# Instance norm on one core: stores and loads in turns on one queue, and the gamma columns and Sqrt table prepared while the first unit lands

## The chip, the cores and the metric

One core of one Trainium2 chip. The time is the device time of one execution in microseconds (us), on the slowest core, which here is the only one. Executions of one kernel agree closely: the kernel before took 626.88 to 627.35 us in its own four runs. A run is called fast when it is not more than 1.5% above the fastest of its kernel, and only fast runs are compared. A ratio of two kernels is the mean time of the one's fast runs over the mean time of the other's fast runs of the same rounds, so it is not quite the ratio of the medians that are quoted beside it.

## The reference

```python
# x: 4 x 8 x 16 x 256 x 256 float32, gamma: 8 x 16 float32
mu    = x.mean(axis=(3, 4), keepdims=True)
var   = ((x - mu) ** 2).mean(axis=(3, 4), keepdims=True)
out   = (x - mu) / np.sqrt(var + 1e-5) * gamma[None, :, :, None, None]
```

Each of 512 channels has 65,536 values, which are normalised by their own mean and variance. 134.22 MB are read and 134.22 MB are written, each value once.

## The kernel before

A *unit* is 16 channels: a tile of 128 partitions x 8,192 float32 (4 MB), eight partitions to a channel. There are 32 units and six slots in SBUF. For each unit VectorE (DVE) sums the rows, ScalarE (ACT) sums the squares, a small matmul adds up the eight partitions of a channel, a few tiny steps give the scale, and DVE normalises the tile in place. Then the tile is stored, and a load that reuses its slot is issued.

```python
    def load(u, queue):
        queue.dma_start(out=slots[u % AHEAD][:], in_=xv[u])       # AHEAD = 6

    for u in range(AHEAD):
        load(u, nc.scalar if u in (1, 3) else nc.sync)
        if u == 1:
            nc.sync.dma_start(out=g_row[:], in_=gv[None, :])
    # ... constants cut
    for u in range(U):                                            # U = 32
        t = slots[u % AHEAD]
        nc.vector.reduce_sum(out=st[:, u, 0:1], in_=t[:], axis=AX.X)
        square = nc.scalar.activation(out=junk[:], in_=t[:], func=ACTF.Square,
                                      accum_out=st[:, u, 1:2])
        if u == 0:
            gamma_columns()              # a copy, 8 matmuls, a copy
        # ... matmul ps, nvar, Sqrt std, reciprocal rstd, scale cut
        nc.vector.tensor_scalar(out=t[:], in0=t[:], scalar1=ps[:, 0:1],
                                scalar2=scale[:, u : u + 1], op0=ALU.add, op1=ALU.mult)
        nc.scalar.dma_start(out=ov[u], in_=t[:])
        if u + AHEAD < U:
            load(u + AHEAD, nc.sync)
```

So all stores go out on the ACT queue, and all loads but two on the SP queue. A load waits until the store of the unit that had its slot six units earlier has landed.

Of the kernel before, what the change touches and what calls it, by code (L numbers as in the profile page):

```python
# [1 line left out]

# [4 lines left out]

F32 = mybir.dt.float32
U8 = mybir.dt.uint8
ALU = mybir.AluOpType  # L10
ACTF = mybir.ActivationFunctionType
AX = mybir.AxisListType


@with_exitstack
def kernel(
    ctx: ExitStack,
    tc: tile.TileContext,
    x: bass.AP,
    gamma: bass.AP,  # L20
    out: bass.AP,
):
    nc = tc.nc
    B, G, C, H, W = x.shape
    P = nc.NUM_PARTITIONS
    HW = H * W
    n_ch = B * G * C
    S = 8
    K = P // S
    F = HW // S  # L30
    U = n_ch // K
    NG = (G * C) // K
    AHEAD = 6
    assert HW % S == 0 and (G * C) % K == 0

    xv = x.rearrange("b g c h w -> (b g c h w)").rearrange("(u p f) -> u p f", p=P, f=F)
    ov = out.rearrange("b g c h w -> (b g c h w)").rearrange("(u p f) -> u p f", p=P, f=F)
    gv = gamma.rearrange("g c -> (g c)")

    data = ctx.enter_context(tc.tile_pool(name="data", bufs=1))  # L40
    singles = ctx.enter_context(tc.tile_pool(name="singles", bufs=1))
    psum = ctx.enter_context(tc.tile_pool(name="psum", bufs=4, space=bass.MemoryType.PSUM))
    ctx.enter_context(tc.manual_schedule())

    slots = [data.tile([P, F], F32, name=f"xt{i}") for i in range(AHEAD)]

    def load(u, queue):
        queue.dma_start(out=slots[u % AHEAD][:], in_=xv[u])  # L48


    g_row = singles.tile([1, G * C], F32, name="g_row")
    for u in range(AHEAD):
        load(u, nc.scalar if u in (1, 3) else nc.sync)
        if u == 1:
            nc.sync.dma_start(out=g_row[:], in_=gv[None, :])


    eps_t = singles.tile([P, 1], F32, name="eps_t")
    nc.gpsimd.memset(eps_t[:], 1e-5)
    one = singles.tile([1, 1], F32, name="one")  # L60
    nc.gpsimd.memset(one[:], 1.0)
    navg = singles.tile([P, K, S], F32, name="navg")
    nc.gpsimd.memset(navg[:], -1.0 / HW)  # L63
    nc.gpsimd.affine_select(  # L64
        out=navg[:], in_=navg[:], pattern=[[-S, K], [0, S]], compare_op=ALU.is_ge,
        fill=0.0, base=0, channel_multiplier=1,
    )
    nc.gpsimd.affine_select(  # L68
        out=navg[:], in_=navg[:], pattern=[[S, K], [0, S]], compare_op=ALU.is_ge,
        fill=0.0, base=S - 1, channel_multiplier=-1,  # L70
    )
    navg_w = navg[:].rearrange("p k s -> p (k s)")
    g_rep = singles.tile([1, NG, K, S], F32, name="g_rep")
    g_ps = psum.tile([P, NG], F32, name="g_ps", bufs=1)
    g_col = singles.tile([P, NG], F32, name="g_col")

    def gamma_columns():
        nc.vector.tensor_copy(  # L78
            out=g_rep[:],
            in_=g_row[:].rearrange("o (n k) -> o n k", n=NG).unsqueeze(3).to_broadcast([1, NG, K, S]),  # L80
        )
        for n in range(NG):
            nc.tensor.matmul(  # L83
                out=g_ps[:, n : n + 1],
                lhsT=g_rep[:, n].rearrange("o k s -> o (k s)"),
                rhs=one[:],
                start=True, stop=True,
            )
        nc.vector.tensor_copy(out=g_col[:], in_=g_ps[:])  # L89

    junk = singles.tile([P, F], U8, name="junk")

    st = singles.tile([P, U, 2], F32, name="st")
    nvar = singles.tile([P, U], F32, name="nvar")
    std = singles.tile([P, U], F32, name="std")
    rstd = singles.tile([P, U], F32, name="rstd")
    scale = singles.tile([P, U], F32, name="scale")

    squares = []
    for u in range(U):  # L100
        t = slots[u % AHEAD]
        nc.vector.reduce_sum(out=st[:, u, 0:1], in_=t[:], axis=AX.X)  # L102
        square = nc.scalar.activation(  # L103
            out=junk[:], in_=t[:], func=ACTF.Square, accum_out=st[:, u, 1:2],
        )
        if u:

            tc.declare_no_dep(square.ins, squares[-1].ins, reason="junk, ordered by the root between")
        squares.append(square)
        if u == 0:  # L110
            gamma_columns()
        ps = psum.tile([P, 2], F32, name="ps")
        nc.tensor.matmul(out=ps[:], lhsT=navg_w, rhs=st[:, u], start=True, stop=True)  # L113
        nc.vector.tensor_scalar(  # L114
            out=nvar[:, u : u + 1], in0=ps[:, 0:1], scalar1=ps[:, 0:1],
            scalar2=ps[:, 1:2], op0=ALU.mult, op1=ALU.add,
        )
        nc.scalar.activation(  # L118
            out=std[:, u : u + 1], in_=nvar[:, u : u + 1], func=ACTF.Sqrt,
            bias=eps_t[:], scale=-1.0,  # L120
        )
        nc.vector.reciprocal(out=rstd[:, u : u + 1], in_=std[:, u : u + 1])  # L122
        g = u % NG
        nc.vector.tensor_mul(  # L124
            out=scale[:, u : u + 1], in0=rstd[:, u : u + 1], in1=g_col[:, g : g + 1],
        )
        nc.vector.tensor_scalar(  # L127
            out=t[:], in0=t[:], scalar1=ps[:, 0:1], scalar2=scale[:, u : u + 1],
            op0=ALU.add, op1=ALU.mult,
        )  # L130
        nc.scalar.dma_start(out=ov[u], in_=t[:])
        if u + AHEAD < U:
            load(u + AHEAD, nc.sync)


# [1 line left out]
_INS = ['x', 'gamma']  # L137
_OUTS = [((4, 8, 16, 256, 256), 'float32')]


# [23 lines left out]
```

## Time and profile before

626.95 us (median of three runs). The profiled execution has a span of 625.1 us.

| | before |
|---|---|
| busy share of the span: DVE, ACT, PE | 71%, 38%, 3% |
| share of the 16 DMA engines' span, both queues | 52.8% + 46.8% |
| mean rate over the span | 429 GB/s |
| DVE work for one unit, and the interval between units late in the run | about 15 us, 19.35 us |

The lines below are from the page of the kernel before: the busy share of the DMA engines (in tenths; 9 is 90% or more) and the rate in 40 slices of the span, the queue table (queue, kind: packets, MB, share of the 16 engines' span), four groups of instructions (count, busy us and mean ns, then the idle time before them) and the issues (KB each, median us from issue to landing). Queue q10 is ACT's, q1 is SP's.

```profile
DMA  8999999999999999999999999999999999999998
GB/s 371 434 436 419 419 436 436 436 436 436 435 436 435 428 426 436 426 436 436 434 436 436 434 434 432 428 432 426 436 436 434 436 436 434 434 436 428 428 436 359
DMA packets 9220, 268.46 MB, mean 429 GB/s; under 512 B 1025, under 2 KB 1026, under 8 KB 1026
...
q10 hardware_dynamic: 4896, 142.61, 52.8%
q1 hardware_dynamic: 4322, 125.83, 46.8%
...
L102 DVE TENSOR_REDUCE st<-xt 128x1 f32<-128x8192 f32 x32 | 277.9, 8684 | 110.2 <-DMA xt<-in_x_dram 110.2
...
L127 DVE TENSOR_SCALAR xt<-xt,ps,scale 128x8192 f32<-128x8192 f32 x32 | 145.6, 4550 | 1.2
...
L118 ACT ACT_TABLE_LOAD x1 | 1.3, 1283 | 6.8 <-DVE nvar L114 6.8
...
L103 ACT ACT_TABLE_LOAD x1 | 1.3, 1283 | 1.7 <-PEq L148 1.7
...
out_dram<-xt ACTq DMA_DIRECT2D x32, 4096.0 KB, 64.1
xt<-in_x_dram SPq DMA_DIRECT2D x30, 4096.0 KB, 29.0
```

Read them together: the transfers fill the run from end to end, and no compute engine comes near that. The only way to be faster is to lose less at the start, at the end, or inside the stream of packets.

Two lines of the timeline show when the first unit is handled (start us, us, engine, line, operation, and the idle time before):

```profile
22.61 8.69 DVE L102 TENSOR_REDUCE st<-xt 128x1 f32<-128x8192 f32 x1 [22.61 <-DMA xt<-in_x_dram]
...
38.51 4.55 DVE L127 TENSOR_SCALAR xt<-xt,ps,scale 128x8192 f32<-128x8192 f32 x1
```

### The profile page before, as it was taken

What the parts mean: (1) busy time and instruction counts of PE and PEld (TensorE: products, weight loads), DVE (VectorE), ACT (ScalarE), POOL (GpSimd) and SP (SyncE); (2) the same over time, 40 slices, a digit from 0 to 9 for tenths busy, and PEclk for the clock granted to TensorE, in tenths of its full rate; (3) what the DMA queues carried; (4) which work ended last, traced back from release to release, by engine and by line L of the source; (5) the groups of instructions that cost most, each with busy time, mean ns of one, the idle gap of its engine ahead of it and who ended that gap; (6) DMA issues with size and microseconds to landing.
All of it is one profiled execution on the core that took longest, in us unless ns stands there. A gap on an engine that the chain in (4) does not pass through costs nothing.

```text
span 625.1 us, 628 instructions
## 1 busy us (share of the span) xinstructions
PE 21.4 (3%) x80; PEld 19.5 (3%) x80; DVE 442.9 (71%) x162; ACT 239.9 (38%) x98; POOL 1.3 (0%) x9
## 2 busy tenths in 40 slices
PE   0020000000000000000000000000000000000000
PEld 0020000000000000000000000000000000000000
DVE  0569999999898767867668676686766877667710
ACT  0435555544444423444224442244432444323400
POOL 0000000000000000000000000000000000000000
DMA  8999999999999999999999999999999999999998
GB/s 371 434 436 419 419 436 436 436 436 436 435 436 435 428 426 436 426 436 436 434 436 436 434 434 432 428 432 426 436 436 434 436 436 434 434 436 428 428 436 359
DMA packets 9220, 268.46 MB, mean 429 GB/s; under 512 B 1025, under 2 KB 1026, under 8 KB 1026
## 3 DMA queue, kind: packets, MB, share of 16 engines
q10 hardware_dynamic: 4896, 142.61, 52.8%
q1 hardware_dynamic: 4322, 125.83, 46.8%
q14 instruction: 2, 0.02, 0.0%
HBM read 134.22 MB, written 134.22 MB: 429 GB/s over the span
## 4 chain that ended last, share of the span: by engine, by line
DMA 62%; DVE 30%; PE 2%; issue 1%; ACT 1%; SPq 0%; ACTq 0%
DMA xt<-in_x_dram 55%; DVE st L102 24%; DMA out_dram<-xt 7%; DVE xt L127 5%; PE ps L113 2%; DVE nvar L114 1%; PE g_ps L83 1%; ACT std L118 0%; ACT L118 0%; DVE rstd L122 0%; DVE scale L124 0%; DVE g_rep L78 0%; SPq L48 0%; ACTq L118 0%
## 5 line engine op out<-in xcount | busy, mean ns | idle before, releaser
L102 DVE TENSOR_REDUCE st<-xt 128x1 f32<-128x8192 f32 x32 | 277.9, 8684 | 110.2 <-DMA xt<-in_x_dram 110.2
L103 ACT ACTIVATE junk<-xt 128x8192 uint8<-128x8192 f32 x32 | 224.9, 7030 | 266.1 <-DMA xt<-in_x_dram 212.1
L127 DVE TENSOR_SCALAR xt<-xt,ps,scale 128x8192 f32<-128x8192 f32 x32 | 145.6, 4550 | 1.2
L118 ACT ACTIVATE std<-nvar,eps_t 128x1 f32<-128x1 f32 x32 | 9.4, 295 | 76.0 <-DVE nvar L114 76.0
L113 PE MATMUL ps<-st,navg 128*128 128x2 f32 x64 | 17.9, 349 | 536.4 <-DVE st L102 536.4
L113 PEld LDWEIGHTS ps<-st,navg 128*128 128x128 f32 x64 | 16.0, 311 | 538.2 <-issue 538.2
L114 DVE TENSOR_SCALAR nvar<-ps 128x1 f32<-128x1 f32 x32 | 9.2, 286 | 23.4 <-PE ps L113 23.4
L122 DVE RECIPROCAL rstd<-std 128x1 f32<-128x1 f32 x32 | 5.2, 164 | 12.9 <-ACT std L118 12.9
L103 ACT ACTIVATION_READ_ACCUMULATOR junk<-xt 128x1 f32 x32 | 6.0, 186 | 0.0
L124 DVE TENSOR_TENSOR scale<-rstd,g_col 128x1 f32<-128x1 f32 x32 | 5.1, 159 | 1.1
L83 PE MATMUL g_ps<-one,g_rep 1*128 1x1 f32 x16 | 3.5, 346 | 32.0 <-DVE g_rep L78 32.0
L83 PEld LDWEIGHTS g_ps<-one,g_rep 1*128 1x128 f32 x16 | 3.5, 325 | 32.0 <-issue 32.0
L118 ACT ACT_TABLE_LOAD x1 | 1.3, 1283 | 6.8 <-DVE nvar L114 6.8
L89 DVE COPY g_col<-g_ps 128x8 f32<-128x8 f32 x1 | 0.2, 166 | 3.7 <-PE g_ps L83 3.7
L103 ACT ACT_TABLE_LOAD x1 | 1.3, 1283 | 1.7 <-PEq L148 1.7
L78 DVE COPY g_rep<-g_row 1x1024 f32<-1x1024 f32 x1 | 0.7, 670 | 0.0
L64 POOL TENSOR_SCALAR_AFFINE_SELECT navg<-navg 128x128 f32<-128x128 f32 x1 | 0.4, 405 | 0.1
L68 POOL TENSOR_SCALAR_AFFINE_SELECT navg<-navg 128x128 f32<-128x128 f32 x1 | 0.4, 399 | 0.1
L63 POOL MEMSET navg<- 128x128 f32 x1 | 0.2, 222 | 0.0
L148 POOL MEMSET const-bfloat16-1.0<- 128x1 bf16 x1 | 0.1, 102 | 0.0
L148 POOL MEMSET const-uint8-127<- 128x1 uint8 x1 | 0.1, 102 | 0.0
L148 POOL MEMSET const-float32-0.0<- 128x1 f32 x1 | 0.1, 99 | 0.3 <-issue 0.3
(3 smaller groups left out, 0.3 us busy)
## 6 DMA issues: line engine op xcount, KB each, us to landing
out_dram<-xt ACTq DMA_DIRECT2D x32, 4096.0 KB, 64.1
xt<-in_x_dram SPq DMA_DIRECT2D x30, 4096.0 KB, 29.0
xt<-in_x_dram ACTq DMA_DIRECT2D x2, 4096.0 KB, 31.4
g_row<-in_gamma_dram SPq DMA_DIRECT2D x1, 0.5 KB
```

The source lines that it names most:

```text
L64: nc.gpsimd.affine_select(out=navg[:], in_=navg[:], pattern=[[-S, K], [0, S]], compare_op=ALU.is_ge, fill=0.0, base=0, channel_multiplier=1,)
L68: nc.gpsimd.affine_select(out=navg[:], in_=navg[:], pattern=[[S, K], [0, S]], compare_op=ALU.is_ge, fill=0.0, base=S - 1, channel_multipli ...
L78: nc.vector.tensor_copy(out=g_rep[:], in_=g_row[:].rearrange("o (n k) -> o n k", n=NG).unsqueeze(3).to_broadcast([1, NG, K, S]),)
L83: nc.tensor.matmul(out=g_ps[:, n : n + 1], lhsT=g_rep[:, n].rearrange("o k s -> o (k s)"), rhs=one[:], start=True, stop=True,)
L102: nc.vector.reduce_sum(out=st[:, u, 0:1], in_=t[:], axis=AX.X)
L103: square = nc.scalar.activation(out=junk[:], in_=t[:], func=ACTF.Square, accum_out=st[:, u, 1:2],)
L113: nc.tensor.matmul(out=ps[:], lhsT=navg_w, rhs=st[:, u], start=True, stop=True)
L114: nc.vector.tensor_scalar(out=nvar[:, u : u + 1], in0=ps[:, 0:1], scalar1=ps[:, 0:1], scalar2=ps[:, 1:2], op0=ALU.mult, op1=ALU.add,)
L118: nc.scalar.activation(out=std[:, u : u + 1], in_=nvar[:, u : u + 1], func=ACTF.Sqrt, bias=eps_t[:], scale=-1.0,)
L122: nc.vector.reciprocal(out=rstd[:, u : u + 1], in_=std[:, u : u + 1])
L124: nc.vector.tensor_mul(out=scale[:, u : u + 1], in0=rstd[:, u : u + 1], in1=g_col[:, g : g + 1],)
L127: nc.vector.tensor_scalar(out=t[:], in0=t[:], scalar1=ps[:, 0:1], scalar2=scale[:, u : u + 1], op0=ALU.add, op1=ALU.mult,)
```

## The change

Its intent: keep loads and stores in one strict order, so that neither runs ahead of the other, and take the gamma columns and the Sqrt table load out of the first unit's way.

```diff
-    def load(u, queue):
-        queue.dma_start(out=slots[u % AHEAD][:], in_=xv[u])
+    def load(u):
+        nc.sync.dma_start(out=slots[u % AHEAD][:], in_=xv[u])

-    for u in range(AHEAD):
-        load(u, nc.scalar if u in (1, 3) else nc.sync)
-        if u == 1:
-            nc.sync.dma_start(out=g_row[:], in_=gv[None, :])
+    nc.scalar.dma_start(out=g_row[:], in_=gv[None, :])
+    for u in range(AHEAD - 1):
+        load(u)
 ...
+    nc.scalar.activation(out=root_eps[:], in_=eps_t[:], func=ACTF.Sqrt)
+    # the body of gamma_columns() stands here now, in front of the loop
 ...
-        if u == 0:
-            gamma_columns()
 ...
-        nc.scalar.dma_start(out=ov[u], in_=t[:])
-        if u + AHEAD < U:
-            load(u + AHEAD, nc.sync)
+        nc.sync.dma_start(out=ov[u], in_=t[:])
+        if u + AHEAD - 1 < U:
+            load(u + AHEAD - 1)
```

The SP queue now holds load 0 to load 4, store 0, load 5, store 1, load 6 and so on.

## The prediction

> **What bounds the kernel now.** The transfers. The page's queue table gives 52.8% + 46.8% = 99.6% of the 16 engines' span, 268.46 MB at a mean 429 GB/s. DVE is busy 71%, ACT 38%. By the timeline a unit takes DVE about 15 us (8.69 reduce, 4.55 normalise, small steps) of the 19.35 us between units late in the run.
>
> By the trace's DMA records each engine moves 512 packets of 32 KB. The first starts at 2.0 us, the last round at 621.8. The period per packet is 1,210.2 ns with three kinds of queueing alike: two queues of loads (22 to 41 us), loads on one and stores on the other (80 to 560 us), stores alone on one queue (after 584 us). So a second queue buys no rate. The floor is 2.0 + 512 x 1.2102 = 621.6 us, plus about 2.3 us until the last store is seen to be complete: 624 us, against a span of 625.1. Only some 1.2 us is lost: 0.6 us in the very first packets (up to 2,032 ns) and 0.65 us in load packets at 44.7 to 48 us, just when the first store starts (up to 1,872 ns).
>
> The Trainium skill, "DMA: Bandwidth & Descriptors", section "Issuing engines are not separate DMA queues", says that DMAs run on the same 16 engines whoever issues them, and that more issuers save only issue time. The trace agrees (1,210 ns with one queue or two; an issue costs 0.33 us).
>
> **What the change moves.**
> - Unit 0 lands alone, at about 12 us (estimate: 2.0 + 8 x 1.21 + 0.6) instead of 22.6.
> - The gamma columns and one of two 1.28 us table loads leave unit 0's chain (reduce ends 31.3, nvar starts 36.1): about 6 us. Unit 0 is normalised near 28 us instead of 43.1. But loads are queued to about 50 us, so the transfers gain nothing.
> - Stores and loads stand in one FIFO. Load u+6 waits for store u to land; behind store u are load u+5 and store u+1, about 17 us of work after 2 us latency, so the engines don't run dry. DVE doesn't hold the FIFO either: eight transfers (77 us) lie between load u+1 and store u+1.
> - All engines now read for 9.7 us, then write for 9.7 us. Pure stretches of each kind ran at full rate before; the turn between them inside one queue is not shown. That is the risk.
>
> **Critical path.** Almost none of the saving is on it. At best the 0.65 us at the first store vanishes.
>
> **Prediction: 626.4 us, 8 in 10 between 625.4 and 629.0.** Faster by over 2%: 0.01; within 2%: 0.93; slower: 0.06.
>
> **What would show it.** Queue table: nearly all bytes on the SP queue, again about 99.6%, mean 428 to 430 GB/s. First DVE reduce at about 12 us, first normalise over near 28. One table load instead of two. Issue to landing: stores about 38 us instead of 64, loads still about 29. DVE and ACT busy times unchanged. Packet period 1,210 ns, no dip at the turns.
>
> **What would make it wrong.** Each turn costing time: 0.2 us at 64 turns adds 13 us and passes 2%. An engine gap at the boundary of two transfers of one queue. SP blocked so long that the queue empties (the rate would dip every 19 us). A faster result needs packets below 1,210 ns, which nothing shows.

## The result

631.98 us, median of four runs (631.34 to 632.25), against 626.93. The ratio is 1.0078, with a 95% interval of 1.006 to 1.0095. That is within 2%, as forecast, but about 5 us slower and 3 us above the upper end of the stated range. The profiled run has a span of 630.1 us, 5.0 more than before.

The answering lines of the page after:

```profile
DMA  8999999999999999999999999999999999999996
GB/s 366 433 435 416 431 422 435 429 431 435 420 431 437 424 435 419 433 437 431 439 431 433 433 433 422 435 435 435 433 433 433 435 433 433 433 433 433 433 433 289
DMA packets 9221, 268.46 MB, mean 426 GB/s; under 512 B 1025, under 2 KB 1026, under 8 KB 1026
...
q1 hardware_dynamic: 9216, 268.44, 99.3%
...
L102 DVE TENSOR_REDUCE st<-xt 128x1 f32<-128x8192 f32 x32 | 277.9, 8684 | 108.9 <-DMA xt<-in_x_dram 108.9
...
L125 DVE TENSOR_SCALAR xt<-xt,ps,scale 128x8192 f32<-128x8192 f32 x32 | 145.6, 4551 | 1.2
...
L73 ACT ACT_TABLE_LOAD x1 | 1.3, 1283 | 1.4 <-PEq L146 1.4
...
xt<-in_x_dram SPq DMA_DIRECT2D x32, 4096.0 KB, 29.3
out_dram<-xt SPq DMA_DIRECT2D x32, 4096.0 KB, 38.9
```

And of the timeline after:

```profile
13.16 8.69 DVE L102 TENSOR_REDUCE st<-xt 128x1 f32<-128x8192 f32 x1 [6.55 <-DMA xt<-in_x_dram]
...
23.64 4.55 DVE L125 TENSOR_SCALAR xt<-xt,ps,scale 128x8192 f32<-128x8192 f32 x1
```

Everything on the compute side came as intended: the first unit is ready at 28.2 us instead of 43.1, and one table load is left. The transfers are just as full, by the share of busy time (99.3%). But a packet that is held up counts as busy all the while, so that share can't show the loss. The rate can: 426 instead of 429 GB/s, and the last slice fell from 359 to 289.

The end of the run shows the loss most plainly. The view by stretches of time gives from:to, length, busy times of the engines, clock, DMA share and GB/s. First the kernel before, then the kernel after:

```profile
612.00:620.00 8.00, 0.00 (x0) 0.00 (x0) 0.00 (x0) 0.00 (x0) 0.00 (x0) 1.00 1.00 430
620.00:622.00 2.00, 0.00 (x0) 0.00 (x0) 0.00 (x0) 0.00 (x0) 0.00 (x0) 1.00 1.10 475
622.00:624.00 2.00, 0.00 (x0) 0.00 (x0) 0.00 (x0) 0.00 (x0) 0.00 (x0) 1.00 0.12 49
624.00:626.00 2.00, 0.00 (x0) 0.00 (x0) 0.00 (x0) 0.00 (x0) 0.00 (x0) 1.00 0.03 8
626.00:628.00 2.00, 0.00 (x0) 0.00 (x0) 0.00 (x0) 0.00 (x0) 0.00 (x0) 1.00 0.00 0
```

```profile
620.00:622.00 2.00, 0.00 (x0) 0.00 (x0) 0.00 (x0) 0.00 (x0) 0.00 (x0) 1.00 1.06 459
622.00:624.00 2.00, 0.00 (x0) 0.00 (x0) 0.00 (x0) 0.00 (x0) 0.00 (x0) 1.00 0.95 410
624.00:626.00 2.00, 0.00 (x0) 0.00 (x0) 0.00 (x0) 0.00 (x0) 0.00 (x0) 1.00 0.34 147
626.00:628.00 2.00, 0.00 (x0) 0.00 (x0) 0.00 (x0) 0.00 (x0) 0.00 (x0) 1.00 0.27 115
```

Packets are counted where they start, so single stretches can pass 1.00. What counts is the shape: before, the last packet of the stores is over by 623.6 us. After, by the packets' own start and length, 11 of the 16 engines still work at 624 us, 6 at 626 and 3 at 628. The 16 DMA engines have come apart.

The trace's landing records tell how far. The Trainium skill, "DMA: Bandwidth & Descriptors", section "Why a DMA increments its semaphore by 16 and not by 1", says that each of the engines that carry a transfer posts its own increment when its share has landed. The trace agrees: each of the 64 large transfers has 16 landing records. The *spread* of a transfer is the time from its first to its last record. This table gives the spread, in us, of the transfer that had landed last by the time named:

```
                by 50   100   150   200   250   300   400   500 us   at the end   last store landed, first and last engine
before          1.72  0.34  0.32  1.01  0.95  0.86  0.90  0.86       0.87         623.07  623.94
after           0.64  1.18  1.56  2.86  2.97  3.91  4.98  4.98       4.97         623.97  628.94
```

With this the 5.0 us are accounted for: the first engine finishes 0.90 us later than before, the last one 4.10 us further behind it (4.97 less 0.87), and from the last landing to the end of the program it is 1.13 us in both.

What puts the engines apart? Not idle time: between 20 and 620 us an engine stands without a packet for about 0.01 us in all, in both kernels, so neither an empty queue nor a gap between two transfers costs anything. The packets themselves take longer. Nearly every packet of 32 KB takes 1,213 ns in both kernels. Call one *stretched* when it took over 1,240 ns, and add up what it took over 1,213, divided by 16 engines. Before, that is 1.26 us: 0.58 in the first packets of the run and 0.63 just when the first store begins. After, it is 3.86 us: 0.69 at the start, 0.92 at the first store, and 2.25 in later groups. The groups lie at 70, 89, 109, 128, 148, 167, 186 us and so on, 19 us apart, and stop after 384 us; after that only one packet is stretched. Those are the *turns*: the places in the queue where a store follows a load, 28 in all. Following each engine's packets up to the record that ends a transfer, the 178 stretched packets after 20 us are:

```
last packet of a load         133
last but one of a load         37
other packets of a load         7
packets of a store              1
```

So it is a load's last packets that are held up, and practically never a store's. An explanation that fits: the engine that is late at a turn is the one that still reads while the others write; it is held up, and is later still at the next turn. This runs on until the engines are so far apart that they no longer turn together, and then it stops. The slowest engine sets the end.

The packets bear out part of this. At the turns from 89 to 148 us, the later an engine begins the last packet of its load, the more that packet is stretched (correlation 0.8 to 0.9). At the later turns this no longer holds: there the very last engines often go through with 1,213 ns, and those a little ahead of them are held up. And not every stretched packet can blame other engines' stores. The 24 at the first store were all due to end before any engine had begun it. At the other turns this is so for 29 of 152, which carry 0.27 of 2.24 us.

### The profile page after: what moved, and what is told of

It is laid out like the page before. It is cut to its first block, busy times and chain, and to the rows that moved or that the text cites. A ratio compares the mean times of both kernels' runs of the same rounds, so it can differ in the third digit from the quotient of the medians.

```text
span 630.1 us, 604 instructions
## 1 busy us (share of the span) xinstructions
PE 21.4 (3%) x80; PEld 19.5 (3%) x80; DVE 443.2 (70%) x162; ACT 238.1 (38%) x98; POOL 1.3 (0%) x9
## 3 DMA queue, kind: packets, MB, share of 16 engines
q1 hardware_dynamic: 9216, 268.44, 99.3%
## 4 chain that ended last, share of the span: by engine, by line
DMA 73%; DVE 20%; PE 1%; ACT 0%; issue 0%; SPq 0%
DMA out_dram<-xt 43%; DMA xt<-in_x_dram 30%; DVE st L102 15%; DVE xt L125 4%; PE ps L111 1%; DVE nvar L112 1%; ACT std L116 0%; DVE rstd L120 0%; DVE scale L122 0%; SPq L49 0%
## 6 DMA issues: line engine op xcount, KB each, us to landing
xt<-in_x_dram SPq DMA_DIRECT2D x32, 4096.0 KB, 29.3
out_dram<-xt SPq DMA_DIRECT2D x32, 4096.0 KB, 38.9
```

## The experiments

Theory A is the explanation just given: engines that turn together hold up the late ones and so drift apart. Rival B: each turn inside one queue costs an engine time by itself, whatever the others do. Rival C: the early preparation or the five loads ahead disturb the transfers, and the queue has nothing to do with it. In the shares and spreads below, "after" is the changed kernel.

### 1. Only the preparation

Before, with only the gamma columns, the Sqrt table and the gamma load moved to the front. Queues, six loads ahead and order stay as before.

```diff
-        if u == 1:
-            nc.sync.dma_start(out=g_row[:], in_=gv[None, :])
+    nc.scalar.dma_start(out=g_row[:], in_=gv[None, :])     # ahead of the loads
+    nc.scalar.activation(out=root_eps[:], in_=eps_t[:], func=ACTF.Sqrt)
+    # gamma columns in front of the loop
```

> Before with only the gamma columns and the Sqrt table moved to the front; queues, loads ahead and order of transfers as before. Theory A (the load-to-store turns of the one queue cost the 5 us, all 16 engines turning at about the same time): no turns here, so 626.9 us within 0.5, landing spread of the last store under 1 us. Rival C (the early preparation or the earlier first unit disturbs the transfers): about 632 us.

Measured: 626.99 us against 627.15, ratio 0.9999 (0.9984 to 1.0014). Final spread 0.80 us. This half of the change is worth nothing and costs nothing.

### 2. Only the queue of the stores put back

```diff
# against after
-        nc.sync.dma_start(out=ov[u], in_=t[:])
+        nc.scalar.dma_start(out=ov[u], in_=t[:])
```

> After, with the stores alone put back on the ACT queue; loads on SP, five ahead. Theory A and rival B (each turn inside one queue costs an engine time, whatever the others do): loads and stores alternate packet by packet, so 626 to 627 us, stretched packets only at the start and at the first store, spread under 1.2 us. Rival C (five loads ahead instead of six, or the early start): stays near 632 us.

Measured: 627.48 us against 627.15, ratio 1.0006 (0.9991 to 1.0021); the expected upper end was 627. Stretched packets: 0.79 us when the first store begins, in loads on the SP queue, and 0.18 us later. The last store's spread is 0.80 us, and the end of the run has the shape of before:

```profile
622.00:624.00 2.00, 0.00 (x0) 0.00 (x0) 0.00 (x0) 0.00 (x0) 0.00 (x0) 1.00 0.42 180
624.00:626.00 2.00, 0.00 (x0) 0.00 (x0) 0.00 (x0) 0.00 (x0) 0.00 (x0) 1.00 0.04 8
626.00:628.00 2.00, 0.00 (x0) 0.00 (x0) 0.00 (x0) 0.00 (x0) 0.00 (x0) 1.00 0.00 0
```

The expectation of a spread under 1.2 us failed in between, where it stood at 2.0 to 2.2 us for most of the run without growing. Rival C falls: the five loads ahead and the early start are still in this kernel. 4.5 of the 5 us hang on having stores and loads in one queue; the rest is not clear of noise. With two queues, the trace shows each engine taking a load packet and a store packet in turn: between 80 and 560 us this is so for 4,802 of the 4,805 packets whose follower is certain.

### 3. Halves of 64 partitions: a miss

To have twice as many turns, each store and load in the loop was split in two.

```diff
# against after
+        v = u + AHEAD - 1
+        for h in (slice(0, P // 2), slice(P // 2, P)):
+            nc.sync.dma_start(out=ov[u][h], in_=t[h])
+            if v < U:
+                nc.sync.dma_start(out=slots[v % AHEAD][h], in_=xv[v][h])
```

> After, with each store and load in the loop split into two transfers of 64 partitions, taken in turns, so twice as many turns, 4.84 us apart. Rival B (a fixed price per turn): twice the loss, about 636 us. Theory A (stalls only while the engines turn together; they stop once the engines are spread over about half a transfer): spread stops near 2.5 us instead of 5, about 629 us.

Measured: 787.10 and 787.33 us in its two fast runs; two more were slow and are left out. Neither theory has this. The page's rate fell at once when the loop's transfers began:

```profile
GB/s 384 441 369 272 285 337 305 314 347 319 367 396 407 399 394 387 360 339 367 355 354 377 352 340 354 347 334 337 320 330 332 320 339 317 314 317 348 364 355 77
```

42% of its 32 KB packets took over 1,240 ns. The Trainium skill, "SBUF — State Buffer", section "Door 1: The DMA port swizzle", says that 64 neighbouring partitions reach only 8 of the 16 ports. That fits, but no run here tests it: 16 engines would crowd on half the ports. The split had changed more than the number of turns, so it says nothing about the theories and was done again along the columns (experiment 5).

### 4. Pairs: half as many turns

```diff
# against after
-        nc.sync.dma_start(out=ov[u], in_=t[:])
-        if u + AHEAD - 1 < U:
-            load(u + AHEAD - 1)
+        if u % 2:
+            nc.sync.dma_start(out=ov[u - 1], in_=slots[(u - 1) % AHEAD][:])
+            nc.sync.dma_start(out=ov[u], in_=t[:])
+            for v in (u + AHEAD - 2, u + AHEAD - 1):
+                if v < U:
+                    load(v)
```

> After, with two stores and then two loads in the queue, so half as many turns, 38.7 us apart. Rival B (a fixed price per turn): half the loss, about 629.5 us. Theory A: the stall of each turn is as large while the engines turn together, and they may spread up to 10 us; with only 16 turns the spread at the end is 3 to 8 us and the time 630 to 635 us, and it has not stopped growing when the run ends.

Measured: 632.06 us, ratio 1.0082 (1.0063 to 1.0101). The spread was 1.54 us by 200 us, 3.05 by 300, 4.29 by 500, and 5.39 at the end. 15 turns instead of 28, and the same loss: rival B's 629.5 us is out, and theory A's range holds, the growth to the end of the run included. The mean over the engines tells less against B: after the first store, the stretched packets add up to 1.05 us an engine here and to 2.25 in after, so they did fall with the number of turns. The time didn't, because the slowest engine sets it.

### 5. Halves of the columns: twice as many turns

```diff
# against after
+        v = u + AHEAD - 1
+        for h in (slice(0, F // 2), slice(F // 2, F)):
+            nc.sync.dma_start(out=ov[u][:, h], in_=t[:, h])
+            if v < U:
+                nc.sync.dma_start(out=slots[v % AHEAD][:, h], in_=xv[v][:, h])
```

> The halves run again, but halved along the columns, so that each transfer keeps all 128 partitions (16 KB packets); the halves run put all 16 engines on 64 partitions at once and so measured something else. Twice as many turns as after, 4.84 us apart. Rival B (a fixed price per turn): about 636 us. Theory A (stalls only while the engines turn together, until they are spread out): spread stops near 2.5 us, about 629 us; at most 5 us and 632 us. Nothing like 800 us.

Measured: 632.91 us, ratio 1.0097 (1.008 to 1.0114). The spread grew to 3.44 us by 200 us and 3.66 by 400, and was 4.12 at the end. The first engine ended at 626.11 us, 2.1 us later than after's: the packets are now 16 KB and take 611 ns each, more than half of 1,213, and there are twice as many. So the time is above theory A's upper figure largely for a reason that is not the turns. Rival B fails again: with twice the turns (55) it would have to lose twice as much. The spread is smaller than after's instead, and the stretch of the 16 KB packets (those over 640 ns, against 611) is 0.84 us an engine, not twice 2.25. Theory A's guess that the spread stops at half a transfer, near 2.5 us, was wrong: it stopped at 3.66.

### 6 and 7. Half of the engines made late from the start: a spoiled control

Four useless loads of 8 partitions go first on the SP queue, once in the kernel before (6) and once in after (7). The Trainium skill, "DMA: Bandwidth & Descriptors", section "Why a DMA increments its semaphore by 16 and not by 1", says that a transfer of 8 partitions runs on 8 engines, the lowest-numbered; the traces have 32 more semaphore packets, 8 for each of the four loads. Which engines they are, the trace doesn't tell. The 4.8 us of the expectations is four packets of 1.21 us on each of the 8.

```diff
# in both, ahead of the first loads
+    for i in range(4):
+        h = slice(8 * i, 8 * i + 8)
+        nc.sync.dma_start(out=slots[AHEAD - 1][h], in_=xv[AHEAD - 1][h])
```

> Control: before, with four useless loads of 8 partitions first on the SP queue[...]. In before the engines are full all the time, so the added packets show in full: 626.9 + 4.8 = 631.8 us under every theory.

> After, with the same four useless loads: half the engines turn from loads to stores 4.84 us behind the other half from the start. Theory A (the loss is engines that turn together pushing each other apart until they are 5 us apart): they start nearly 5 us apart, so few stalls are left; the added work is nearly free against after: 631 to 633.5 us, spread 5 to 6.5 us. Rival B (a price per turn, or a cause that acts on each engine alone): the added work adds in full, 636.5 us, spread near 10 us.

Measured: 645.86 us for before with these loads (ratio 1.0298) and 643.98 for after with them (1.0267). The control missed its sum by 14 us, and run 7 missed theory A's range by over 10 and rival B's 636.5 by 7: many of the first packets took 3 to 4.5 us instead of 1.21. (With the rows set apart, in runs 11 and 12, none took over 3.) Still, the kernel with turns, which is 0.8% slower without the useless loads, is no slower than the control with them. As the two starts differ (one queue or two), the totals prove little. The trace of run 7 proves more. Its first large load already has a spread of 4.31 us, close to where after's spread stops. From 20 us on, its stretched packets add up to 0.08 us an engine, against 3.17 in after; the stall at the first store is missing too. The spread ended at 5.96 us, within A's 5 to 6.5 and not near B's 10. Engines that are out of step from the start are spared, as theory A says and rival B doesn't.

### 8 to 10. Which side of the memory

Three looks with one run each, so their state is unknown and only their traces are used. Run 8 is the base: after with five slots, which leaves room for a spare tile. In run 9 the stores go to the spare tile in SBUF, in run 10 the loads copy a tile that lies in SBUF. Their outputs are wrong, which doesn't matter for the times.

```diff
# 8, 9 and 10, against after
-    AHEAD = 6
+    AHEAD = 5
# 9
+    sink = data.tile([P, F], F32, name="sink")
-        nc.sync.dma_start(out=ov[u], in_=t[:])
+        nc.sync.dma_start(out=ov[u] if u >= U - 3 else sink[:], in_=t[:])
# 10
+    well = data.tile([P, F], F32, name="well")
+    nc.sync.dma_start(out=well[:], in_=xv[AHEAD - 1])
-            load(u + AHEAD - 1)
+            nc.sync.dma_start(out=slots[(u + AHEAD - 1) % AHEAD][:], in_=well[:])
```

> Base for the next two: after with five slots instead of six, loads four ahead. The queue order is the same, so under both theories as after: about 632 us, spread about 5 us at the end, stretched packets at the turns to stores.

> Wrong result on purpose: all stores but the last three go to a spare tile in SBUF, loads still come from HBM. Theory A1 (the turn stalls because many engines begin to write HBM at once): no stretched packets at the turns, spread stays under 1.2 us. Theory A2 (the stall lies in the turn from writing SBUF to reading it, or in the engines' own pipeline): stretched packets at the turns remain, and the engines spread to several us.

> Wrong result on purpose: from unit 4 on the loads copy a tile that lies in SBUF, stores go to HBM as in after. Theory A1 (many engines begin to write HBM at once): stretched packets at the turns to stores remain, about 0.9 us at the first, and the engines spread by several us. Theory A3 (it is the turn of HBM itself from reading to writing): nothing reads HBM here, so no stretched packets and spread under 1.2 us.

```
spread, us      by 50   100   150   200   250   300   400   500 us   at the end   time
8 five slots    0.69  0.90  2.50  3.56  4.15  4.66  4.72  4.67       4.72         631.21
9 to SBUF       0.54  0.49  0.49  1.28  1.31  1.30  1.32  1.35       1.43         629.26
10 from SBUF    0.45  0.49  0.49  1.22  9.40 19.47 22.70 22.69      12.80         739.67
```

The base does what after does. With the stores going to SBUF, the engines go on turning in step after the first store, with a spread of about half a us in the first 150 us, and hardly a packet is stretched at a later turn. So theory A2 (the turn inside SBUF, or the engines' own pipeline) is out; the one step at 160 us is there in several runs and comes with a small transfer of instructions. Run 9 is nevertheless slower than before, as its packets have a period of 1,214.8 ns instead of 1,210.6 (80 to 560 us) and the first store's stall is there (0.95 us). With the loads coming from SBUF and the stores going to HBM, the engines also turn together up to 160 us without a stretched packet at the later turns, so theory A1 (many engines beginning to write HBM is enough) is out. What both lack, and the kernel after has, is loads from HBM against stores to HBM. That is A3: the turn of the HBM traffic from reading to writing. It rests on one run of each kind, of unknown state. The first store's stall is in both runs (1.02 us in run 10), so it need not have the same cause as the drift. After 200 us run 10 fell into something else: the spread ran up to 22 us and the time to 739.67. Its cause is open.

### 11 and 12. The offset again, on separate ports

The rows of the four useless loads are now 12 partitions apart.

```diff
# against 6 and 7
-        h = slice(8 * i, 8 * i + 8)
+        h = slice(i, i + 96, 12)
```

> The offset control again, mended: the rows of the four useless loads are 12 partitions apart, because eight neighbouring partitions crowded the packets to 3 to 4.5 us. Now each should be one packet of 1.21 us on each of 8 engines, 4.84 us in all. In before the engines are always full: 626.9 + 4.8 = 631.8 us under every theory (631 to 633).

> After with the same mended loads. Theory A (engines that turn from HBM loads to HBM stores together stall and so spread until they are out of step): half the engines start 4.8 us late, few stalls are left, so the useless work is nearly free: 631 to 633.5 us, within 0.3% of after itself and of the control, spread 5 to 6.5 us. Rival B (every turn costs an engine time by itself): 636 to 637 us, spread near 10 us, stalls at the turns as in after.

Measured: 637.09 us for the control (ratio 1.0169) and 637.38 for after (1.016), so the two are equal. The expected sums failed again: the added work cost the control 10 us, not 4.8, because the first transfers of the run still crowded one another. And the offset did not come out as meant: in run 12 the first large load had a spread of 2.31 us only. From there it grew, with stretched packets at the turns (3.07 us in sum), to 4.66 us by 200 us, and hardly after that (4.85 at the end). The time of run 12 lies just above rival B's stated range, but that range reckoned with 4.8 us of added work; with the control's 10 us, B would need 642. So the pair is no clean test by its totals. What it adds is a third starting point: from 0.64, 2.31 and 4.31 us (after, 12 and 7) the spread went to 4.97, 4.85 and 5.96.

### 13. A try at beating both

```diff
# against run 1
+    zeros = singles.tile([P, 128], F32, name="zeros")
+    nc.vector.memset(zeros[:], 0.0)
+    nc.scalar.dma_start(out=ov[U - 1][:, 0:128], in_=zeros[:])
     nc.scalar.dma_start(out=g_row[:], in_=gv[None, :])
```

> Tries to beat both: the hoist-only kernel with a small store of 64 KB put first (128 columns of the last unit, written over by that unit's own store later). In every run so far the first store stretched the packets then in flight once by 0.64 to 1.1 us an engine, even where it went to SBUF. If that is a price of first use, the early store pays it while the first loads also start: no stretch near 44 us, 626.3 us (ratio 0.999). If it is the turn from loads to stores, the stretch near 44 us stays and the time is 626.9 to 627.5 us.

Measured: 627.64 us against 627.07, ratio 1.001 (0.9998 to 1.0023). The stretch when the first large store begins stayed (0.75 us). A small early store doesn't pay for it, so it isn't a price of the first write to HBM as such. (The expectation says that every run had this stall. Run 7 had not.) No version beat the kernel before. By the prediction's own sum the floor of the span is about 624 us, and the kernel before is at 625.1.

## Why the prediction was right or wrong

- **What bounds the kernel: right.** The transfers, before and after; all compute groups kept their times (DVE 442.9 and 443.2 us).
- **The preparation is off the critical path: right.** The first unit was ready at 28.2 us ("near 28"), and run 1 shows a worth of nothing (0.9999).
- **The FIFO doesn't run dry: right.** Stores land 38.9 us after issue ("about 38"), loads 29.3 ("about 29"). The DMA row of the page has no slice below nine tenths between the first and the last. (The first reduce began at 13.2 us, not "about 12".)
- **"The period per packet is 1,210.2 ns with three kinds of queueing alike [...] So a second queue buys no rate": the step that failed.** All three kinds were measured truly. But none of them has all engines turning from HBM loads to HBM stores together, and the sum set nothing for it: "At best the 0.65 us at the first store vanishes". The term "turn" was put at 0 and measured 5.0 us: 0.9 for the first engine to finish and 4.1 of spread. The stall at the first store, which the prediction hoped to lose, grew from 0.63 to 0.92 us. It could have been a hint: the one place in the old trace where a pure read stream met its first store, with stretched packets on the load queue. But run 9 has this stall without the later ones, so the two may differ in cause.
- **The risk was named, with the wrong shape.** "Each turn costing time: 0.2 us at 64 turns adds 13 us." There are 28 turns to a store; turns back to a load cost nothing that the trace shows; and the loss is no price per turn. 15 turns lose as much (run 4), 55 don't lose twice (run 5), and engines out of step have almost no stretched packets (run 7). In after, the stalls end once the spread is near 5 us, which fits a loss of 5 us and not 13.
- **"Again about 99.6%, mean 428 to 430 GB/s": wrong.** 99.3% and 426.

Shown: one queue for both directions is the cause (run 2 against after); nearly all packets that are held up are the last ones of a load; the engines drift apart and the last one sets the end. Supported by single runs: it needs HBM on both sides (runs 8 to 10). Argued, and only in part borne out: that the late engine is held up because the others already write. Open: what inside the memory or the DMA engines holds a late load back; why the drift stops near 5 us, and near 3.7 with half transfers; why the first store of a run stalls all engines alike, even with SBUF as its target, and not in run 7; and the collapse of run 10.

## What to carry to other kernels

When a kernel is bound by transfers and each DMA engine is full, look at the slowest of the 16 engines, not at the mean: compare the first and the last landing record of a transfer, and the rate in the last few microseconds. Leave large loads from HBM and large stores to HBM on two queues: here they then mixed packet by packet, and the 5 us of drift did not arise. A fixed order in one queue keeps every transfer on schedule and still loses time, and taking steps off the first unit's chain is worth nothing while loads are queued past it.

## What the Trainium skill lacked or had wrong

- "DMA: Bandwidth & Descriptors", section "Issuing engines are not separate DMA queues": it says that issuing from several engines only saves issue time. Here the choice of queue alone made the difference between 627.48 and 631.98 us (run 2 and after), with no issue time on the line.
- The same page has no word on a load's last packets being stretched (up to 2.2 us for 1.21) where a store follows in the same queue, nor on engines drifting apart (spread 0.6 to 5.0 us). No page has it.
- The same page, section "Where 436 GB/s comes from": its warning says that for transfers between HBM and SBUF the HBM side, about 358 GB/s, binds. For a core that works alone this does not hold: the trace has 436 GB/s in many slices and 429 in the mean, near the 435 of the fabric. The skill does not lack the right number, as the same warning calls a measured 425 GB/s near fabric rate; the sentence lacks the condition.
- "SBUF — State Buffer", section "Door 1: The DMA port swizzle": its 8 ports for 64 partitions fit run 3, but its figure of about 218 GB/s for 64 partitions is for one transfer at a time. A queue with loads and stores of 64 partitions in turns ran at a mean of 342 GB/s.
- No page has the collapse of run 10 (copies inside SBUF between stores to HBM: 739.67 us, spread up to 22.7 us).
